# Retention's v turned at eviction, residual's copies beside attention, and more steps ahead of three uses

## The chip, the cores and the metric

The kernel runs on one core of one Trainium2 chip. A core has a matrix engine (TensorE, PE in the profile), a vector engine (VectorE, DVE), a scalar engine (ScalarE, ACT), GpSimd (POOL) and SyncE (SP), which issues most of the DMAs. The metric is the device time of one execution in microseconds. The profile's own execution is one of its own, beside the timed runs.

## The reference

One layer of a hybrid encoder over 1024 positions of width 2048, in float32. An RMSNorm of x is multiplied with one input matrix; its columns are retention's q, k, v and gate (8 heads of 128 each) and attention's q (8 heads), k, v (2 heads) and gate. The two branches are gated, put side by side, multiplied with an output matrix and added to x; a last RMSNorm follows.

```python
h = rms_norm(x, norm_w)
proj = h @ w_in
rq, rk, rv, rg, aq, ak, av, ag = jnp.split(proj, splits, axis=-1)
y_ret = retention_branch(rq, rk, rv, decay_fwd, decay_bwd, gn_w, gn_b) * silu(rg)
y_att = window_attention_branch(aq, ak, av, sink) * silu(ag)
return rms_norm(x + concat([y_ret, y_att]) @ w_out, final_norm_w)
```

Retention works on chunks of 128 positions, in both directions. Per head and chunk it needs the masked scores q k^T times v (`inner`), a running state that sums k^T v over the chunks with a decay (`kv_chunk`, `step`), and q times the state of the chunks before (`cross`). A GroupNorm over each head's 128 values follows.

## The kernel before, in words

**The projection sets the time.** It is a Strassen-like scheme: a unit is 512 columns of the input matrix and one half (part) of the sum over 2048 inputs, and it takes 7 products, listed in `PRODUCTS`. Each product of 4 x 2 groups of three float32r matmuls (`mm3`, L99 to L101) writes two PSUM banks. `PHASES` gives the order of the units: first part 0 of akv, aq0, aq1, rk0, rq0 (attention's k, v and q, and half of retention's k and q); then part 1 of these and of rv0, rk1, rq1, rv1; then part 0 of rv0, rk1, rq1, rv1 and of the gates; then part 1 of the gates. So retention's v, in rv0 (heads 0 to 3) and rv1 (heads 4 to 7), is made in two passes. `evict` takes a product from PSUM: for products 1, 6, 5 and 4 ScalarE copies the bank into a tile `ct` (L317), for 2, 7 and 3 VectorE adds the bank to a held tile (L92). Four of the seven give a finished quarter, which `store` puts into the list `stores`; `flush` issues them, in the last of the next product's four steps. The first pass writes plainly on SyncE's queue (L285), the second adds in memory on GpSimd's queue (L287). The tiles `ct` come from a ring of 8.

**Steps and jobs.** All else runs beside the projection as generators. `advance` counts one step of the projection (six matmuls of width 512) and then lets each job run up to its next `yield`; `idle(n)` is n steps. So the order of TensorE's, SyncE's and GpSimd's instructions is written out by hand: the jobs' instructions stand where their step is. `manual_schedule` names just these three engines. The instructions of VectorE and ScalarE are ordered by the planner of the Tile framework, which works through a simulated time and may put a later one first when it takes its inputs to be there; only `behind(...)` holds an instruction in the written order. Every engine then works through its own list in order.

**Jobs that matter here.** `attention` starts behind akv in phase 1 and, when its eight heads are done, runs `retention` and then `gating` as one job. `settled` counts a block as ready 8 steps after its last unit, which is also the time in which its stores land. `turn_v` (L752) fetches each v head 1 to 7 as two halves from `pr`, turns each on VectorE in blocks of 32x32 (`turn_half`, L152) and stores it into `vz`. `residual` (L1204) copies x into `res`, eight copies of 1 MB from memory to memory, one every 12 steps; the output projection adds on to `res` later.

**A retention head** (`head`). It waits until kT and qT are loaded and rotated (`fetch`, L779 to L796: load, rest some steps, then per half multiply, multiply, add on VectorE). It takes the scores (L840), waits for its v and until the head before is normalised (`while busy`), transposes kT (L567) into k_tok, starts the next head's kT, scales v (L859), forms the outer products (L872) and on VectorE the states (L884, L886), which are split into a rounded part and a rest, sH and sL (L88, L85). Then q is split (qhl), the next head's qT is started, and after an `idle` come `inner` (L920) and `cross`, which multiplies qhl with sH and sL (`mm3`) and adds it to y (L913). `normed` normalises y, turns it (L147), and stores it into `mix`. Head 0's v is no case of `turn_v`: `fetch_v` loads it and TensorE transposes it. The other heads' `fetch_v` is a `gather` of four DMAs (L161) from `vz`.

**Behind it.** `gating` loads `mix` and the gates, multiplies them (L1330 for attention's half, L1328 for retention's) and splits the operands (c) of the output projection, which begins when the last unit is done.

Of the kernel before, what the change touches and what calls it, by code (L numbers as in the profile page):

```python
# [9 lines left out]
F32 = mybir.dt.float32  # L10
# [8 lines left out]
P = 128  # L19
SQ = 32  # L20
S = 1024
# [4 lines left out]
RH = 8  # L26
# [17 lines left out]
BLOCKS = {  # L44
    "akv": 5120, "aq0": 4096, "aq1": 4608, "ag0": 5632, "ag1": 6144,
    "rk0": 1024, "rk1": 1536, "rq0": 0, "rq1": 512, "rv0": 2048, "rv1": 2560, "rg0": 3072, "rg1": 3584,
}
T_RQ, T_RK, T_RV, T_RG, T_AQ, T_AK, T_AV, T_AG = 0, 8, 16, 24, 32, 40, 42, 44
# [10 lines left out]
def hybrid_layer_kernel(  # L59
# [6 lines left out]
    nc = tc.nc  # L66
    x, w_in, w_out, out = x[0], w_in[0], w_out[0], out[0]
# [12 lines left out]
    def ax():  # L80
        return psp.tile([P, HALF], F32, name="ax", tag="ax", bufs=4)
# [9 lines left out]
    def add(dst, a, b):  # L91
        nc.vector.tensor_tensor(out=dst, in0=a, in1=b, op=ALU.add)  # L92
# [10 lines left out]
    def behind(it, ins):  # L103

        if it:
            tc.keep_in_program_order(ins)

    def blk(i, n=1):
        return slice(i * P, (i + n) * P)

    def half(i):
        return slice(i * HALF, (i + 1) * HALF)
# [9 lines left out]
    def start(job):  # L122
        if next(job, True) is None:
            jobs.append(job)
# [4 lines left out]
    def idle(n):  # L129
        for _ in range(n):  # L130
            yield
# [8 lines left out]
    pr = [dram.tile([P, S], F32, name=f"pr{i}") for i in range(52)]  # L140
    mix = [dram.tile([P, S], F32, name=f"mix{i}") for i in range(KT)]
    vz = [dram.tile([2, P, HALF], F32, name=f"vz{i}") for i in range(RH)]
    NB = P // SQ
# [6 lines left out]
    def turn_half(dst, src):  # L150

        nc.vector.transpose(out=dst.rearrange("p (b c i) -> p b c i", b=NB, i=SQ), in_=src.rearrange("p (c b i) -> p b c i", b=NB, i=SQ))  # L152

    def gather(dst, src):

        if len(src.shape) == 3:
            of = src.rearrange("m (a i) (b r) -> b i (m a) r", i=SQ, b=NB)
        else:
            of = src.rearrange("(a i) (b r) -> b i a r", i=SQ, b=NB)
        for b in range(NB):  # L160
            nc.sync.dma_start(out=dst[b * SQ:(b + 1) * SQ].rearrange("p (n r) -> p n r", r=of.shape[-1]), in_=of[b])  # L161

    def in_order(t):

        return t.rearrange("p (a c j) -> p c a j", a=NB, j=SQ)
# [19 lines left out]
    def ct():  # L185
        return wp.tile([P, HALF], F32, name="ct", tag="ct", bufs=8)
# [90 lines left out]
    done, seen = set(), set()  # L277
    comb = {}

    stores = []  # L280
# [29 lines left out]
    def evict(b, i, a, bank, held):  # L310

        def store(n, m, t):
            stores.append((b not in seen, pr[BLOCKS[b] // P + 2 * n + a][:, half(m)], t))

        if i in (1, 6, 5, 4):
            t = ct()
            nc.scalar.copy(out=t, in_=bank)  # L317
            if i == 4:
                store(1, 0, t)
            else:  # L320
                held[i, a] = t
        else:
            t = held.pop(({2: 1, 7: 5, 3: 6}[i], a))
            add(t, bank, t)
            store(*{2: (0, 0), 7: (1, 1), 3: (0, 1)}[i], t)
# [8 lines left out]
    def first_block(b, of):  # L334
# [3 lines left out]
        for m, order in ((0, QUARTERS), (1, QUARTERS[2:] + QUARTERS[:2])):  # L338
            for n, k in order:
# [30 lines left out]
                t += 1  # L370
        seen.add(b)
        on_done(0, b)

    def project(on_done, on_free):
# [187 lines left out]
    def transposed(src):  # L562

        for b in range(2):
            pt = ax()
            for t in range(4):
                nc.tensor.transpose(pt[:, blk(t)], src[:, blk(b * 4 + t)], ident)  # L567
            yield b, pt
# [5 lines left out]
    def settled(b):  # L574
        return b in done and clock[0] >= since[b] + 8

    def needs(*blocks):

        while not all(settled(b) for b in blocks):
            yield  # L580
# [166 lines left out]
        nc.vector.tensor_scalar(out=kd, in0=kd, scalar1=SCALE, scalar2=None, op0=ALU.mult)  # L747


    turned = set()  # L750

    def turn_v():  # L752
        for h in range(1, RH):
            yield from needs("rv" + str(h // 4))
            for m in range(2):
                f, z = ct(), ct()
                nc.sync.dma_start(out=f, in_=pr[T_RV + h][:, half(m)])
                yield from idle(6)
                turn_half(z, f)
                yield from idle(3)  # L760
                nc.sync.dma_start(out=vz[h][m], in_=z)
                yield
            turned.add(h)

    def retention():
        with right("ret") as ret:
            df = ret.tile([P, P], F32, name="df")
# [4 lines left out]
            kq, vs = {}, {}  # L772
# [3 lines left out]
            def fetch(name, c, h):  # L776

                t = ret.tile([P, S], F32, name=name, tag=name)
                nc.sync.dma_start(out=t, in_=pr[c + h])  # L779
                beside = []  # L780

                def pair(i):
                    beside.append(ret.tile([P, HALF], F32, name="rx", tag="sd" if h == 0 and c == T_RQ else "rx", bufs=2))
                    for r in (0, HP):
                        nc.sync.dma_start(out=beside[i][r:r + HP], in_=pr[c + h][HP - r:P - r, half(i)])

                for i in range(2):
                    pair(i)
                yield from idle(7 if h or c == T_RK else 11)
                for i in range(2):  # L790
                    u, b = t[:, half(i)], beside[i]
                    behind(h == 0, nc.vector.tensor_tensor(out=u, in0=u, in1=rot[:, 0, half(i)], op=ALU.mult))
                    yield
                    behind(h == 0, nc.vector.tensor_tensor(out=b, in0=b, in1=rot[:, 1, half(i)], op=ALU.mult))
                    add(u, u, b)
                    yield  # L796
                kq[name, h] = t

            def fetch_v(h):
                if h == 0:  # L800
                    yield from needs("rv0")
                    f = ret.tile([P, S], F32, name="vT", tag="vdq")
                    nc.sync.dma_start(out=f, in_=pr[T_RV])
                    yield from idle(5)
                    t = ret.tile([P, S], F32, name="v_tok")
                    for b, pt in transposed(f):
                        nc.scalar.copy(out=t[:, half(b)], in_=pt)
                        yield
                    vs[h] = [t[:, half(m)].rearrange("p (c a j) -> p c a j", a=NB, j=SQ) for m in range(2)]
                    return  # L810
                while h not in turned:
                    yield
                t = ret.tile([P, S], F32, name="v_tok")
                gather(t, vz[h])
                yield from idle(5)
                vs[h] = [in_order(t[:, half(m)]) for m in range(2)]

            def next_of(name, c, h):

                if h < RH:  # L820
                    yield from idle(2)
                    yield from needs(("rk" if c == T_RK else "rq") + str(h // 4))
                    yield from fetch(name, c, h)

            def head(h):
# [10 lines left out]
                for b in range(2):  # L836
                    sc = ax()
                    for t in range(4):
                        c = blk(4 * b + t)
# [57 lines left out]
                y = ret.tile([P, NT, P], F32, name="y", tag="y")  # L897
                bn = ret.tile([P, NT, 6], F32, name="bn")
                mv = ret.tile([P, NT, 2], F32, name="mv")
                yield from idle(2)  # L900

                def cross(c0):
                    cr = ax().rearrange("p (c d e) -> p c d e", d=2, e=P)
# [25 lines left out]
                if h + 1 < RH:  # L929
                    yield  # L930
                    start(fetch_v(h + 1))
# [28 lines left out]
            def heads():  # L960
                nc.gpsimd.dma_start(out=rot, in_=rot_r)
                while to_load:
                    yield
                yield from idle(8)
                yield
                start(next_of("kT", T_RK, 0))
                yield from idle(3)
                start(next_of("qT", T_RQ, 0))
                start(fetch_v(0))
                yield  # L970
                for h in range(RH):
                    yield from head(h)
                while len(finished) < RH:
                    yield
# [208 lines left out]
    def on_done(p, b):  # L1183
        if b in done:
            since.setdefault(b, clock[0])
        if p == 1 and b == "akv":
            start(attention())
        if p == 2 and b == "rv0":
            start(turn_v())
        if p == 2 and b == "rq1":  # L1190
            start(residual())


# [10 lines left out]
    def residual():  # L1204

        for t in range(NT):
            nc.sync.dma_start(out=res[t], in_=x[blk(t)])
            yield from idle(12)
# [276 lines left out]
    for u in range(len(OUT)):  # L1485
# [4 lines left out]
        for group in LAST if u == 3 else [(i,) for i in PRODUCTS]:  # L1490
# [13 lines left out]
            for at, (p, t, j, q) in enumerate(order):  # L1504
# [6 lines left out]
                bank, c = (X if p in ON_X else Y), comb[p]  # L1511
# [80 lines left out]
```

## Time and profile before

| | |
|---|---|
| Timed runs | 1531.01, 1532.34, 1531.01 us (median 1531.01) |
| The profiled execution | 1529.65 us, of it a span of 1527.9 us |
| Mean granted TensorE clock | 0.995 |
| TensorE busy | 1503.0 us (98%), 7286 matmul records |
| VectorE busy | 1086.0 us (71%) |
| ScalarE busy | 695.2 us (45%) |
| Attention beside the projection | about 330 to 655 us of the span |
| Retention beside the projection | about 665 to 1105 us |
| Output projection | from about 1211 us |

TensorE's busy share counts a matmul from issue to its modelled end, so matmuls in a row overlap; the spacing of their starts is their price. Where TensorE has idle time, or where its clock is below 1.00, time is lost. VectorE's share is a mean over stages in which it is nearly idle and others in which it never rests.

### The profile page before, as it was taken

The page shows a single profiled execution, that of the slowest core. Times are in us where ns is not written, and L with a number is a line of the kernel's source. Part 1 is how long each engine was busy: PE and PEld are TensorE (multiplying, and loading weights), DVE is VectorE, ACT ScalarE, POOL GpSimd, SP SyncE. Part 2 cuts the span into 40 slices and gives each one's busy share as a digit, 9 for nine tenths or more (in the row PEclk, how much of TensorE's full clock was granted, in tenths as well). Part 3 has the DMA queues.
Part 4 walks back from the last instruction along what each step waited for, and adds up shares of the span by engine and source line. Part 5 has one row for each costly group of instructions (what it writes and reads, how often), then busy time and mean ns, then how long its engine had stood idle before and what let it go on. Part 6 is the DMA issues. An engine that isn't in the chain of part 4 may idle for free.

```text
span 1527.9 us, 20264 instructions
## 1 busy us (share of the span) xinstructions
PE 1503.0 (98%) x7286; PEld 1263.7 (83%) x7286; DVE 1086.0 (71%) x1861; ACT 695.2 (45%) x1141; POOL 149.0 (10%) x169
## 2 busy tenths in 40 slices
PE   9999999999999999999999999999999999999997
PEld 7888888788888888888887888887888878888886
DVE  6896594557767576756977697768755966776766
ACT  7543462334545354533534453444444663542425
POOL 0000001111010000011111100001111102020001
PEclk9999999999999999999999999999999999999999
DMA  8288847889573425796787858589689699394656
GB/s 321 65 284 307 310 165 196 231 197 253 155 207 125 138 83 182 283 309 166 162 203 194 230 164 262 169 268 325 174 234 262 150 217 226 83 212 165 214 175 254
DMA packets 167447, 317.86 MB, mean 208 GB/s; under 512 B 14865, under 2 KB 84913, under 8 KB 158514
## 3 DMA queue, kind: packets, MB, share of 16 engines
q1 hardware_dynamic: 143298, 265.69, 51.9%
q0 software_dynamic: 19728, 36.71, 15.7%
q10 hardware_dynamic: 4320, 14.17, 2.8%
q8 instruction: 57, 0.93, 0.2%
q14 instruction: 44, 0.36, 0.1%
HBM read 196.70 MB, written 128.19 MB: 213 GB/s over the span
## 4 chain that ended last, share of the span: by engine, by line
PE 70%; issue 11%; DVE 11%; DMA 6%; SPq 1%; POOL 1%; ACT 0%; ACTq 0%; DVEq 0%; POOLq 0%
PE pj L101 17%; PE pj L99 17%; PE pj L100 17%; PE ax L100 5%; PE ax L101 5%; PE ax L99 5%; DMA kT<-pr 3%; DVE wL L85 2%; DMA xt<-in_x_dram 1%; DVE ct L92 1%; PE ax L645 1%; DMA pr<-ct 1%; DVE c L85 1%; DVE st L886 1%; DVE sL L85 1%
## 5 line engine op out<-in xcount | busy, mean ns | idle before, releaser
L99 PE MATMUL pj<-c,wH 128*128 128x512 f32 x1444 | 576.3, 399 | 0.0
L101 PE MATMUL pj<-c,wL 128*128 128x512 f32 x1440 | 563.7, 391 | 2.5 <-DVE wL L85 2.5
L100 PE MATMUL pj<-c,wH 128*128 128x512 f32 x1444 | 564.1, 391 | 0.0
L101 PEld LDWEIGHTS pj<-c,wL 128*128 128x128 f32 x1440 | 270.9, 188 | 62.9 <-DVE wL L85 4.8
L100 PEld LDWEIGHTS pj<-c,wH 128*128 128x128 f32 x1444 | 272.3, 189 | 50.5 <-DVE c L1000 0.3
L99 PEld LDWEIGHTS pj<-c,wH 128*128 128x128 f32 x1444 | 272.3, 189 | 50.2 <-issue 0.3
L85 DVE TENSOR_TENSOR wL<-a,wH 128x1024 fp32r<-128x1024 f32 x157 | 191.4, 1219 | 117.0 <-ACT wH L88 114.8
L88 ACT CAST wH<-a 128x1024 fp32r<-128x1024 f32 (+1 forms) x159 | 166.2, 1045 | 216.9 <-PE pj L100 112.0
L317 ACT COPY ct<-pj 128x512 f32<-128x512 f32 x192 | 111.5, 585 | 209.7 <-PE pj L101 208.8
L287 POOL DMA_DIRECT2D pr<-ct x104 | 91.9, 952 | 622.9 <-DVE ct L92 502.4
L92 DVE TENSOR_TENSOR ct<-pj,ct 128x512 f32<-128x512 f32 x164 | 108.9, 685 | 48.6 <-PE pj L101 47.8
L85 DVE TENSOR_TENSOR wL<-s,wH 128x1024 fp32r<-128x1024 f32 x56 | 68.3, 1219 | 50.6 <-ACT wH L88 50.3
L100 PE MATMUL pj<-wL,c 128*128 128x512 f32 x224 | 87.4, 390 | 1.2 <-DVE wL L85 1.1
L99 PE MATMUL pj<-wH,c 128*128 128x512 f32 x224 | 87.2, 389 | 0.0
L101 PE MATMUL pj<-wH,c 128*128 128x512 f32 x224 | 87.1, 389 | 0.0
L100 PE MATMUL ax<-wL,c 128*128 128x512 f32 x208 | 81.2, 390 | 0.1
L101 PE MATMUL ax<-wH,c 128*128 128x512 f32 x208 | 81.0, 389 | 0.0
L99 PE MATMUL ax<-wH,c 128*128 128x512 f32 x208 | 80.9, 389 | 0.0
L88 ACT CAST wH<-s 128x1024 fp32r<-128x1024 f32 x56 | 59.0, 1053 | 22.1 <-DVE s L95 9.9
L88 ACT CAST sH<-st 128x256 fp32r<-128x256 f32 x56 | 22.7, 406 | 76.6 <-DVE st L886 42.2
L100 PEld LDWEIGHTS pj<-wL,c 128*128 128x128 f32 x224 | 42.1, 188 | 10.6 <-DVE wL L85 2.0
L99 PEld LDWEIGHTS pj<-wH,c 128*128 128x128 f32 x224 | 42.1, 188 | 8.8
(246 smaller groups left out, 2036.3 us busy)
## 6 DMA issues: line engine op xcount, KB each, us to landing
a<-in_w_in_dram SPq DMA_DIRECT2D x103, 512.0 KB, 5.9
kept<-c SPq DMA_DIRECT2D x28, 1024.0 KB, 7.9
c<-kept SPq DMA_DIRECT2D x28, 1024.0 KB, 9.3
pr<-ct SPq DMA_DIRECT2D x110, 256.0 KB, 5.6
pr<-ct POOLq DMA_DIRECT2D x104, 256.0 KB, 6.0
a<-in_w_out_dram SPq DMA_DIRECT2D x18, 512.0 KB, 5.2
rx<-pr SPq DMA_DIRECT2D x64, 128.0 KB, 6.8
ysrc<-pr ACTq DMA_DIRECT2D x16, 512.0 KB, 5.9
```

The source lines that it names most:

```text
L85: return nc.vector.tensor_tensor(out=dst, in0=src, in1=high.bitcast(F32), op=ALU.subtract)
L88: behind(pinned, nc.scalar.copy(out=dst_h, in_=src))
L92: nc.vector.tensor_tensor(out=dst, in0=a, in1=b, op=ALU.add)
L99: nc.tensor.matmul(po, aH, bH, start=first, stop=False, **kw)
L100: nc.tensor.matmul(po, aH, bL, start=False, stop=False, **kw)
L101: nc.tensor.matmul(po, aL, bH, start=False, stop=last, **kw)
L287: nc.gpsimd.dma_start(out=dst, in_=t, accum_op=ALU.add)
L317: nc.scalar.copy(out=t, in_=bank)
L645: nc.tensor.transpose(pt[:, blk(j)], s[:, blk(j)], ident)
L886: nc.vector.scalar_tensor_tensor(out=cur[:, d], in0=prev[:, d], scalar=cd[:, d * RH + h:d * RH + h + 1], in1=p, op0=ALU.mult, op1=ALU.add)
```

## The change

There are five edits.

1. `evict`: where a finished quarter belongs to rv0 or rv1, it is turned by `turn_half` into a second `ct` tile, and that is stored, into `vz` instead of `pr`, in the first pass and, adding, in the second.
2. `turn_v` and its start are gone, and `fetch_v` does for head 0 what it does for the others: wait for the block, gather, rest 5 steps.
3. `fetch`: kT rests 10 steps between its load and its rotation where it rested 7; qT keeps its 7 (11 for head 0).
4. `head`: 3 idle steps instead of 2 between the split of q and `inner` and `cross`.
5. `residual` starts when rq0 is done in phase 1 (step 284) instead of rq1 in phase 2 (step 480).

```diff
@@ evict
         def store(n, m, t):
-            stores.append((b not in seen, pr[BLOCKS[b] // P + 2 * n + a][:, half(m)], t))
+            c = BLOCKS[b] // P + 2 * n + a
+            if b in ("rv0", "rv1"):
+                z = ct()
+                turn_half(z, t)
+                stores.append((b not in seen, vz[c - T_RV][m], z))
+            else:
+                stores.append((b not in seen, pr[c][:, half(m)], t))
@@ turn_v
-    turned = set()
-
-    def turn_v():
-        for h in range(1, RH):
-            yield from needs("rv" + str(h // 4))
-            for m in range(2):
-                f, z = ct(), ct()
-                nc.sync.dma_start(out=f, in_=pr[T_RV + h][:, half(m)])
-                yield from idle(6)
-                turn_half(z, f)
-                yield from idle(3)
-                nc.sync.dma_start(out=vz[h][m], in_=z)
-                yield
-            turned.add(h)
@@ fetch
-                yield from idle(7 if h or c == T_RK else 11)
+                yield from idle(10 if c == T_RK else 7 if h else 11)
@@ fetch_v
-                if h == 0:
-                    yield from needs("rv0")
-                    f = ret.tile([P, S], F32, name="vT", tag="vdq")
-                    nc.sync.dma_start(out=f, in_=pr[T_RV])
-                    yield from idle(5)
-                    t = ret.tile([P, S], F32, name="v_tok")
-                    for b, pt in transposed(f):
-                        nc.scalar.copy(out=t[:, half(b)], in_=pt)
-                        yield
-                    vs[h] = [t[:, half(m)].rearrange("p (c a j) -> p c a j", a=NB, j=SQ) for m in range(2)]
-                    return
-                while h not in turned:
-                    yield
+                yield from needs("rv" + str(h // 4))
                 t = ret.tile([P, S], F32, name="v_tok")
                 gather(t, vz[h])
                 yield from idle(5)
@@ head
-                yield from idle(2)
+                yield from idle(3)
@@ on_done
-        if p == 2 and b == "rv0":
-            start(turn_v())
-        if p == 2 and b == "rq1":
+        if p == 1 and b == "rq0":
             start(residual())
```

## The prediction

> **What bounds the kernel now.** I read the page's busy times first.
>
> ```profile
> span 1527.9 us, 20264 instructions
> ...
> PE 1503.0 (98%) x7286; PEld 1263.7 (83%) x7286; DVE 1086.0 (71%) x1861; ACT 695.2 (45%) x1141; POOL 149.0 (10%) x169
> ```
>
> TensorE is busy for 1503.0 of 1527.9 us, so a change can win only the 24.9 us in which it is idle, what a lowered clock costs, and TensorE instructions that go away. The table by stages says where that lies; its columns are the stretch, its length, then busy time and count for PE, PEld, DVE, ACT and POOL, the granted clock, DMA share and GB/s.
>
> ```profile
> 784.00:843.00 59.00, 53.16 (x280) 44.63 (x279) 44.28 (x93) 25.75 (x47) 10.78 (x11) 0.99 0.77 198
> 843.00:894.00 51.00, 50.31 (x264) 42.96 (x263) 38.97 (x87) 21.68 (x39) 2.57 (x1) 0.98 0.67 204
> 944.00:995.00 51.00, 49.63 (x264) 42.31 (x264) 42.77 (x98) 21.41 (x40) 3.05 (x1) 1.00 0.65 202
> 995.00:1048.00 53.00, 51.15 (x262) 43.26 (x261) 41.29 (x95) 22.59 (x41) 2.45 (x1) 0.97 0.86 279
> 1100.00:1150.00 50.00, 50.00 (x222) 41.41 (x221) 30.68 (x31) 21.39 (x29) 8.81 (x10) 1.00 0.79 207
> 435.00:492.00 57.00, 57.00 (x311) 49.95 (x310) 43.60 (x120) 32.38 (x75) 1.74 (x2) 1.00 0.46 139
> 492.00:592.00 100.00, 100.00 (x521) 86.25 (x520) 62.90 (x142) 45.37 (x95) 0.00 (x0) 1.00 0.33 108
> 592.00:647.00 55.00, 55.00 (x294) 48.08 (x293) 40.52 (x108) 29.39 (x67) 0.00 (x0) 1.00 0.77 273
> 1211.00:1234.00 23.00, 21.65 (x93) 16.91 (x92) 22.83 (x21) 13.83 (x17) 1.74 (x2) 1.00 0.98 208
> ```
>
> From 784 to 1048 us retention's heads run beside the projection, and TensorE is idle there for 5.84 + 0.69 + 1.37 + 1.85 = 9.75 us (length less PE busy of the first four rows). The clock below 1.00 costs 59 x 0.01 + 51 x 0.02 + 53 x 0.03 = 3.2 us more. This stage, 13 us, is what the change can win. In attention (435 to 647 us) TensorE never stops. The fifth row gives the step of the text: 50 us for 222 matmuls is 0.225 us each, and a step of the projection is 6 of them, 1.35 us.
>
> Who ends TensorE's waits in retention (690 to 1060 us; total, times, longest), and what VectorE waits for there:
>
> ```profile
> PE ax L100 <- DVE sL L85: 4.2, 5, 1.3
> PE ax L99 <- ACT sH L88: 3.0, 3, 2.1
> PE ax L101 <- DVE qhl L85: 1.6, 2, 0.8
> PE pj L101 <- DVE wL L85: 1.0, 2, 0.5
> ```
>
> ```profile
> DVE kT L792 <- DMA kT<-pr: 30.6, 7, 6.5
> DVE ct L152 <- DMA pr<-ct: 4.3, 1, 4.3
> DVE ct L152 <- DMA ct<-pr: 4.0, 2, 3.7
> DVE qT L792 <- DMA qT<-pr: 3.3, 1, 3.3
> ```
>
> All but 1.0 us is one place: `cross`, where a head's q (qhl) meets its states (sH, sL). Those come late because VectorE stood still, up to 6.5 us, for the next head's kT. The timeline of VectorE shows one such head, that of TensorE its end:
>
> ```profile
> 817.92 1.23 DVE L85 TENSOR_TENSOR wL<-s,wH 128x1024 fp32r<-128x1024 f32 x1 [1.68 <-ACT wH L88]
> 825.65 1.29 DVE L792 TENSOR_TENSOR kT<-kT,rot 128x512 f32<-128x512 f32 x2 [6.50 <-DMA kT<-pr]
> 826.86 0.68 DVE L794 TENSOR_TENSOR rx<-rx,rot 128x512 f32<-128x512 f32 x1
> 827.46 1.28 DVE L92 TENSOR_TENSOR ct<-pj,ct 128x512 f32<-128x512 f32 x2
> 828.66 1.21 DVE L85 TENSOR_TENSOR wL<-a,wH 128x1024 fp32r<-128x1024 f32 x1
> 829.79 0.48 DVE L884 COPY st<-ax 128x128 f32<-128x128 f32 x2
> ...
> 837.09 0.68 DVE L92 TENSOR_TENSOR ct<-pj,ct 128x512 f32<-128x512 f32 x1
> ```
>
> ```profile
> 787.88 0.33 PE L100 MATMUL ax<-sL,qhl 128*128 128x128 f32 x1 [1.31 <-DVE sL L85]
> ...
> 839.12 0.33 PE L99 MATMUL ax<-sH,qhl 128*128 128x128 f32 x1 [2.06 <-ACT sH L88]
> 840.15 0.33 PE L100 MATMUL ax<-sL,qhl 128*128 128x128 f32 x1 [0.71 <-DVE sL L85]
> 841.29 0.33 PE L101 MATMUL ax<-sH,qhl 128*128 128x128 f32 x1 [0.81 <-DVE qhl L85]
> ```
>
> VectorE is idle until 825.65, then works without a break until `cross` is reached at 839. One thing more is to be seen here. In the code the rotation of kT (L792) stands 3 + 7 steps behind the k_tok transposes, the head's state updates (L884) 7 steps behind them. On the chip L792 came first. VectorE's order is the planner's (only TensorE, SyncE and GpSimd are written out by hand), and it put L792 where it thought the load had landed.
>
> **The change part by part.** The sum is made against the profiled execution: 1529.65 us, of which 1527.9 are the span; the median shown is 1531.01, 1.4 above it.
>
> ```profile
> L152 DVE STREAM_TRANSPOSE ct<-ct x14: 682/702/711, 705.7 to 996.9; 128x512 f32<-128x512 f32 x14
> ```
>
> ```profile
> 756.67 0.89 PE ax L840 x8
> ```
>
> ```profile
> L567 PE MATMUL ax<-ident,vT 128*128 128x128 f32 x8 | 1.2, 272 | 0.0
> ```
>
> *Head 0's v.* Its 8 transposes leave TensorE. Eight 128x128 matmuls issued in a row take 0.89 us (the L840 piece), so: -0.9. The two copies on ScalarE and one load go too, and four gathers come in their place, as for every other head. Head 0 gets v two steps earlier.
>
> *No turn_v.* 14 transposes of 0.70 us (9.8 us of VectorE), their 8.3 us of waits, 14 loads and 14 stores on SyncE's queue leave retention. VectorE's order around kT stays, and the waits that were counted are kT's: I take -0.5, with 0 and -3 as bounds (-3 where two turns less per head, 1.4 us, come off the two crossings that stay late).
>
> *Turns at eviction.* 32 transposes of the same shape come: 16 in the first pass of rv0 and rv1, beside attention, 16 in the second. No store or byte is added; each store waits for one more VectorE instruction, on SyncE's queue in the first pass and on GpSimd's in the second, and it uses a second of the 8 `ct` buffers. In the first pass a unit of 55 to 57 us gets 8 x 0.70 = 5.6 us and has 13.4 and 14.5 us of idle VectorE (435 and 592 rows) to hide it. Without that cover it is 11.2 us. The turns come in pairs of 1.4 us ahead of the operands that TensorE wants next, so I take +1, bounds 0 and +5. The second pass of rv1 lies at 784 to 843 us, where nothing is idle once kT has landed: the turns behind the additions of product 7 (827.46) and product 3 (the second of them at 837.09) stand in the burst ahead of 839, 2.8 us, less the removed turn of this head, 0.7: +2.1, bounds 0 and +5.6 (all eight).
>
> *One step more ahead of inner and cross* (idle 2 to 3). TensorE's order is by hand, so `cross` really comes 1.35 us later behind the states and qhl. Each crossing's wait falls by at most that: 1.31 by 1.3, the 3.58 at 839 to 841 by 1.35, and the 0.69, 1.37 and 1.85 us of the other three windows by 0.7, 1.35 and 1.35. Together -6.0. Bounds 0 (VectorE slides as well) and -8.8 (all three kinds). With the waits half of the 3.2 us of lowered clock goes: -1.6, bounds 0 and -3.2. The clock is below 1.00 in three of the windows, though no wait in them is longer than 2.1 us. [...]
>
> *Three more steps for kT.* By hand only the place in the program moves. As the timeline shows, L792 runs long before its place in the program, so the stall that ends at 825.65 stays: 0. The bound is the other reading, below.
>
> *The price of the step.* I counted the steps of `head` from the code. From one k_tok to the next it is 27 before: the chain qhl, idle 2, load of qT, 7 steps, rotation, scores. `normed` frees y at step 26, just ahead of it. With the added step it frees y at 27, so `while busy` holds the next head a step: 28. Head 0 starts two steps sooner (438 for 440), head 7 at 634 for 629, and retention ends at step 665 instead of 659. So `gating`, which follows it, starts 6 x 1.35 = 8.1 us later, while the output projection begins at the same step, 732. This is what gating's end looks like in VectorE's timeline, and the only wait it leaves TensorE with (1200 to 1240 us):
>
> ```profile
> 1175.80 1.23 DVE L1330 TENSOR_TENSOR ysrc<-ysrc,yt 128x1024 f32<-128x1024 f32 x1 [5.83 <-DMA yt<-mix]
> ...
> 1188.76 1.22 DVE L1330 TENSOR_TENSOR ysrc<-ysrc,yt 128x1024 f32<-128x1024 f32 x1
> 1189.90 1.22 DVE L85 TENSOR_TENSOR c<-ysrc,c 128x1024 fp32r<-128x1024 f32 x1
> ...
> 1230.90 1.22 DVE L85 TENSOR_TENSOR wL<-a,wH 128x1024 fp32r<-128x1024 f32 x1
> ```
>
> ```profile
> PE pj L100 <- DVE wL L85: 1.1, 1, 1.1
> ```
>
> From the last product (1188.76) to 1232 VectorE never rests, and TensorE catches up with it. Moved by up to 8.1 us, the block's end moves by less, since other operands fill the hole in front: +3, bounds 0 and +8.
>
> *Residual's copies.* The eight move from 788 to 945 us to behind step 284, one per 12 steps, that is to 435 to about 590 us:
>
> ```profile
> L1207 SPq DMA_DIRECT2D res<-in_x_dram x8: 500/521/713, 787.9 to 944.8; - x8
> ...
> DMA to landing us min/median/max: 7.3/8.5/10.0
> ```
>
> At 8.5 us in 16 to 20 they meet a DMA share of 0.46 and 0.33. Loads behind them on SyncE's queue land later, but the weights are asked for a unit ahead: 0, bounds -1 (kT lands sooner) and +2.
>
> Sum: -0.9 - 0.5 + 1 + 2.1 - 6.0 - 1.6 + 3 = -2.9 by the takings alone. Two of them lean high: the turns in this burst and the late gating are each charged as if no planner moved anything around them. Halving those two, as the middle between bound 0 and the taking, gives -5.4. I forecast between the two, -4.2 us: 1525.4 in the profile, **1526.8 us** in the median.
>
> **The rivals.**
>
> *A. Nothing to be seen.* The waits move rather than go: VectorE still stands for kT, the eviction's turns lengthen the burst by the 2.8 us that the step gives back over two heads, attention pays 2, gating 3. Then -0.9 - 6.0 + 2.8 + 2 + 3 = +0.9, less 0.5 for turn_v and 1.0 of clock: -0.6, 1530.4. For it: the 30.6 us of kT waits are left as they are by my own reading. Against: three of five crossings wait 1.37 us or less, and these vanish with one step.
>
> *B. kT's wait goes as well.* If the planner follows the program, three steps take 4.05 us off each of the seven waits; the rest of 9.75 us (3.7) and of the clock (1.6) would go on top: 1526.8 - 5.3 = 1521.5, and 1517.5 where neither gating nor attention costs its 3 + 1. For it: 30.6 us in 7 heads are 4.4 each, about three steps. Against: L792 ahead of L884 in the timeline. [...]
>
> *C. Slower: gating becomes the bound.* One mechanism, at 1188 to 1240 us: the head's 28th step delays the last product by the full 8.1 us, the 12 operand splits behind it stand ahead of wL in VectorE's order, and TensorE waits all of it at steps 732 to 744. It decides from about 6 us of delay on, if the crossings win less than 4: 1531 + 8 - 4 = 1535. For it: VectorE is 22.83 of 23.00 us busy in the 1211 row. Against: the 5.83 us hole ahead of 1175.80, which a later product leaves free for other operands.
>
> **How the numbers follow.** 0.2%, about 3 us, is what can be told from no change. Forecast 0.40; B 0.14; A 0.28; C 0.18. Faster: forecast and B, less the edge of the forecast near 1528, 0.52. Same: A and that edge, less A's edge, 0.28. Slower: C and A's edge, 0.20. The forecast's own range is 1521 to 1531. To leave out 2 in 10 the range takes B's and C's times with little beyond: 1516 to 1537.
>
> **What would show it.** Right: waits of `ax` on sH, sL and qhl between 690 and 1060 us down from 8.8 to about 3; no L152; L792 still behind 25 to 30 us of kT; scores (L840) of neighbouring heads 28 steps apart; the last L1330 of attention's half some 6 us later, with up to 4 us of wait for wL behind it. Wrong: kT's wait gone (B); waits on wL of 8 us at 1211 to 1240 (C); waits in attention, where there are none now; a second pass of rv1 that stops TensorE for more than its 5.84 us.

## The result, and the profile after

The changed kernel takes 1518.67 us in the median (1518.10 to 1520.17), the kernel before 1531.01 us (1530.22 to 1532.34): ratio 0.992, 95% interval 0.9903 to 0.9937, faster by 12.3 us. The forecast was 1526.8 us, 4.2 us faster. The side is right and the time lies in the stated range of 1516 to 1537 us, but the forecast size is a third of what came.

The page of the changed kernel, its span and busy times:

```profile
span 1516.3 us, 20238 instructions
...
PE 1498.1 (99%) x7278; PEld 1260.4 (83%) x7278; DVE 1097.8 (72%) x1879; ACT 695.9 (46%) x1139; POOL 148.1 (10%) x169
```

Lines have moved: the rotation is L783 now (L792), its scores L819 (L840), `inner` L899 (L920), attention's half of gating L1307 (L1330). The table by stages of the changed kernel (stretch, length, busy time and count of PE, PEld, DVE, ACT, POOL, granted clock, DMA share, GB/s):

```profile
784.00:843.00 59.00, 59.00 (x323) 50.91 (x322) 50.00 (x103) 26.28 (x46) 10.56 (x11) 1.00 0.67 148
843.00:894.00 51.00, 51.00 (x272) 43.55 (x271) 42.27 (x98) 23.11 (x42) 1.66 (x1) 1.00 0.51 155
944.00:995.00 51.00, 51.00 (x270) 43.26 (x269) 42.40 (x96) 22.49 (x40) 1.92 (x1) 1.00 0.52 162
995.00:1048.00 53.00, 53.00 (x283) 45.43 (x282) 45.23 (x92) 25.50 (x46) 6.75 (x4) 1.00 0.92 315
435.00:492.00 57.00, 56.81 (x308) 49.57 (x308) 46.17 (x126) 31.77 (x73) 1.74 (x2) 1.00 0.60 196
1211.00:1260.00 49.00, 44.77 (x190) 36.25 (x189) 24.26 (x25) 25.50 (x29) 5.68 (x7) 0.97 0.91 227
690.00:1060.00 370.00, 370.00 (x1956) 316.06 (x1955) 302.50 (x623) 171.10 (x298) 39.61 (x35) 1.00 0.65 181
```

In retention TensorE no longer stops at all: of its waits between 690 and 1060 us the view has no row left, where before it had 9.8 us, and the clock is 1.00 in all four stretches. Attention loses 0.19 us. A wait behind 1211 us has grown from 1.1 us to 3.7. Who ends VectorE's waits in retention (690 to 1060 us; total, times, longest), and TensorE's behind it (1060 to 1290 us):

```profile
DVE wL L85 <- ACT wH L88: 28.5, 16, 5.4
DVE kT L783 <- DMA kT<-pr: 17.4, 6, 4.9
```

```profile
PE pj L100 <- DVE wL L85: 4.2, 2, 3.7
```

VectorE's stalls for kT have shrunk from 30.6 to 17.4 us, and the 8.3 us for turn_v's loads are gone. Its waits for ScalarE's half of the weight splits (wH) are now the largest, but TensorE stands still for none of them here.

The cleanest account is the place of the output projection's first matmul in TensorE's timeline, first before, then after:

```profile
1211.20 0.39 PE L99 MATMUL ax<-wH,c 128*128 128x512 f32 x1
```

```profile
1195.72 0.39 PE L99 MATMUL ax<-wH,c 128*128 128x512 f32 x1
```

Up to there 1211.20 - 1195.72 = 15.5 us are won. From there to the end of the span it was 1527.9 - 1211.2 = 316.7 us and is 1516.3 - 1195.7 = 320.6, so 3.9 us are given back. The difference is the span's 11.6 us.

### The profile page after: what moved, and what is told of

Read it like the earlier page. It is cut to its first block, busy times and chain, and to the rows that moved or that the text cites. A ratio compares the mean times of both kernels' runs of the same rounds, so it can differ in the third digit from the quotient of the medians.

```text
span 1516.3 us, 20238 instructions
## 1 busy us (share of the span) xinstructions
PE 1498.1 (99%) x7278; PEld 1260.4 (83%) x7278; DVE 1097.8 (72%) x1879; ACT 695.9 (46%) x1139; POOL 148.1 (10%) x169
## 4 chain that ended last, share of the span: by engine, by line
PE 79%; issue 9%; DVE 5%; DMA 5%; ACT 1%; SPq 0%; POOL 0%; ACTq 0%; POOLq 0%; DVEq 0%
PE pj L101 20%; PE pj L100 20%; PE pj L99 20%; PE ax L101 5%; PE ax L100 5%; PE ax L99 5%; PE ax L851 2%; DMA xt<-in_x_dram 1%; DVE wL L85 1%; PE ax L651 1%; DMA pr<-ct 1%; PE ax L819 1%; PE ax L899 1%; DVE c L85 1%; DMA q<-pr 1%
## 5 line engine op out<-in xcount | busy, mean ns | idle before, releaser
L287 POOL DMA_DIRECT2D pr<-ct x88 | 78.0, 957 | 539.2 <-DVE ct L92 412.4
L641 ACT ACTIVATE s<-s,nm 128x385 f32<-128x385 f32 (+1 forms) x64 | 37.6, 589 | 28.5 <-DVE nm L636 25.7
```

Of the source, the lines that this page charges most:

```text
L287: nc.gpsimd.dma_start(out=dst, in_=t, accum_op=ALU.add)
L641: nc.scalar.activation(out=s[:, 0:w + 1], in_=s[:, 0:w + 1], func=AF.Exp, scale=-1.0, bias=nm, accum_out=den)
```

## The experiments

The theories at the start, as the expectations name them. Theory 1: the step ahead of `cross` takes the waits away. Theory 2: fewer transfers and loads on SyncE's queue do it (kT lands earlier, nothing of turn_v stands in VectorE's list), and the step is not needed. Theory 3: kT's longer rest does nothing. Theory 4: the 28-step head makes gating late, and that is the wait behind 1200 us.

Each ratio is to the kernel before, from runs on the same chip; the other columns are read from the one profiled execution of each kernel, which can lie 2 or 3 us from its median, and that of a_copies_late 5 us (1525.02 us, the slowest of its six runs, for a median of 1519.88). "Steps" is the length of a head in steps of the projection; "idle" is length less PE busy of 690 to 1060 us, "output begins" the first matmul as above, "rest" the span less that.

| kernel | steps | ratio, 95% interval | idle | output begins | rest |
|---|---|---|---|---|---|
| before | 27 | 1 | 9.75 | 1211.2 | 316.7 |
| changed | 28 | 0.992 (0.9903-0.9937) | 0.00 | 1195.7 | 320.6 |
| b_step | 28 | 0.9994 (0.9983-1.0006) | 5.32 | 1208.8 | 317.2 |
| b_turn | 27 | 0.9996 (0.9987-1.0006) | 10.50 | 1212.0 | 319.0 |
| b_copies | 27 | 0.9973 (0.9963-0.9984) | 9.04 | 1207.8 | 316.1 |
| b_kt10 | 27 | 1.0011 (1.0000-1.0021) | 10.36 | 1215.4 | 316.4 |
| a_step2 | 27 | 0.9988 (0.9977-0.9999) | 5.70 | 1207.6 | 320.1 |
| a_kt7 | 28 | 0.9936 (0.9912-0.9960) | 1.30 | 1198.2 | 320.3 |
| a_copies_late | 28 | 0.9932 (0.9911-0.9952) | 4.00 | 1202.6 | 320.6 |
| a_norm | 27 | 1.0006 (0.9994-1.0018) | 7.77 | 1211.3 | 319.5 |
| a_per28 | 28 | 0.9962 (0.9949-0.9974) | 4.48 | 1202.6 | 321.5 |
| a_29 | 29 | 1.0026 (1.0012-1.0039) | 3.17 | 1214.8 | 316.1 |
| a_last | 28 | 0.9925 (0.9910-0.9940) | 0.10 | 1197.0 | 322.6 |
| b_gate6 | 27 | 1.0036 (1.0022-1.0050) | 10.06 | 1215.3 | 320.7 |

### One part of the change alone, added to the kernel before

**b_step**, the step alone:

```diff
-                yield from idle(2)
+                yield from idle(3)
```

> The kernel before with the extra step alone (idle 2 to 3 ahead of inner and cross), nothing else. Theory 1 (the step takes the crossings' waits away): waits of ax on sH, sL and qhl between 690 and 1060 us fall from 8.8 to 3 or less, TensorE's wait for wL near 1216 us rises from 1.1 to about 4, and the time is 3 to 6 us below before. Theory 2 (fewer transfers take the waits away, the step is not needed): the waits stay above 5 us, the gating's price of 3 to 5 us comes on top, and the time is at or up to 4 us above before.

The step does to the crossings what the prediction said. TensorE's waits in 690 to 1060 us (total, times, longest), and behind 1060:

```profile
PE ax L100 <- DVE sL L85: 3.1, 4, 1.0
PE pj L101 <- DVE wL L85: 1.7, 3, 0.6
```

```profile
PE pj L101 <- DVE wL L85: 1.8, 1, 1.8
PE ax L100 <- DVE wL L85: 0.8, 1, 0.8
```

Waits on sH, sL and qhl fall from 8.8 to 3.1 us, close to the "about 3" that the prediction named. Yet the time stays: 0.9994. Other waits came, for the projection's own weight splits (wL): behind 1060 us TensorE is idle for 3.76 us where before had 1.35, and behind the wait at 1174.86 the clock is lowered, 0.66 from 1175 to 1180 us (last section). What VectorE waits for changes too, though no load was touched:

```profile
DVE kT L792 <- DMA kT<-pr: 21.5, 6, 6.9
```

Before had 30.6 us here. Theory 1 is right about the place and wrong about the time.

**b_turn**, edits 1 and 2 alone (the diff of `evict`, `turn_v` and `fetch_v` above):

> The kernel before with retention's v turned at eviction and stored turned, no turn_v, head 0's v gathered; the step stays 2, kT's rest 7, residual's copies late. Theory 1 (the step does it): waits of ax on sH, sL and qhl stay at 6 us or more, and the time is within 3 us of before (0.9 us of TensorE's transposes goes in any case). Theory 2 (the relief of SyncE's queue and of VectorE does it): VectorE's waits for kT fall from 30.6 to about 20 us, those waits of ax fall to 3 us or less, and the time is 6 to 10 us below before. My prediction's charge of 2.1 us for the turns in the burst at 784 to 843 us would show as TensorE idle there for more than 5.84 us.

No gain: 0.9996. Its own rows, stage and VectorE's wait, then what TensorE waits for behind 1060 us:

```profile
784.00:843.00 59.00, 54.69 (x295) 46.43 (x294) 47.44 (x102) 26.58 (x47) 11.35 (x11) 1.00 0.75 197
```

```profile
DVE kT L783 <- DMA kT<-pr: 27.8, 7, 7.2
```

```profile
PE pj L100 <- DVE wL L85: 3.2, 1, 3.2
PE pj L101 <- DVE wL L85: 2.4, 2, 1.5
```

The turns in the burst of rv1's second pass cost nothing: 59.00 - 54.69 = 4.31 us idle, below the 5.84 of before. But kT's waits stay (27.8) and the crossings still wait 6.2 us, so theory 2 falls, and the wait of over 3 us for wL behind 1200 us is already there, with 27-step heads and gating as early as before.

**b_copies**, edit 5 alone:

```diff
+        if p == 1 and b == "rq0":
+            start(residual())
...
-        if p == 2 and b == "rq1":
-            start(residual())
```

> The kernel before with residual's eight copies beside attention and nothing else. Theory 2a (the copies slow kT's loads): VectorE's waits for kT fall from 30.6 us by 5 or more, waits of ax fall by 2 to 4 us, time 2 to 5 us below before. Theory 1 and the prediction: kT's waits fall by less than 5 us, time within 1.5 us of before. Either way attention from 435 to 647 us stays without waits.

Faster by 4 us, but not in the way that theory 2a named: kT's waits are 30.0 us, and TensorE's idle time falls by only 9.75 - 9.04 = 0.7 us. The rest is the clock: in the four stretches of the prediction's first rows, b_copies has 1.00 where before has 0.99, 0.98, 1.00 and 0.97. Two stretches behind crossings of before, and the two behind the longest crossing waits of b_copies:

```profile
843.00:846.00 3.00, 3.00 (x12) 2.44 (x11) 3.00 (x7) 0.00 (x0) 0.00 (x0) 0.66 0.97 231
1040.00:1044.00 4.00, 4.00 (x14) 3.20 (x13) 4.00 (x11) 0.00 (x0) 0.00 (x0) 0.62 1.00 263
```

```profile
841.00:845.00 4.00, 4.00 (x25) 3.51 (x25) 4.00 (x8) 0.03 (x1) 0.81 (x1) 1.00 0.98 178
988.00:992.00 4.00, 4.00 (x25) 3.55 (x24) 4.00 (x16) 0.00 (x0) 0.00 (x0) 1.00 0.53 157
```

In these stretches before has a clock near 0.64, b_copies 1.00. The matmul counts can't be compared, since b_copies' stretches hold narrower matmuls as well; the spacing of the projection's 128x512 matmuls can, first before, then b_copies:

```profile
843.72 0.63 PE L100 MATMUL pj<-c,wH 128*128 128x512 f32 x1
844.15 0.63 PE L101 MATMUL pj<-c,wL 128*128 128x512 f32 x1
```

```profile
842.11 0.39 PE L101 MATMUL pj<-c,wL 128*128 128x512 f32 x1
842.33 0.40 PE L99 MATMUL pj<-c,wH 128*128 128x512 f32 x1
```

They start 0.43 us apart in the one and about 0.23 in the other. At the two crossings behind which the clock of before fell, b_copies waits less: 0.71 + 0.81 = 1.5 us for 3.58 (839 to 841 us), and 0.81 for 1.86 (1035 to 1038 us). But its own longest crossing wait, 1.20 + 0.77 = 1.97 us at 985 and 986 us, is longer than the 1.86 of before and leaves the clock alone. Why is not explained by any row.

**b_kt10**, kT's rest 7 to 10:

```diff
-                yield from idle(7 if h or c == T_RK else 11)
+                yield from idle(10 if c == T_RK else 7 if h else 11)
```

> The kernel before with kT's rest raised from 7 to 10 steps and nothing else. Theory 3 (the planner has put the rotation ahead of its place in the program anyway): the rotation stands at the same place of VectorE's order for heads 1 to 6, VectorE's waits for kT stay at 27 us or more, time within 1.5 us of before. Rival B of the prediction: each of seven waits is 4.05 us shorter, kT's waits fall below 10 us, time about 5 us below before.

```profile
DVE kT L792 <- DMA kT<-pr: 31.6, 7, 7.4
```

Theory 3 holds: 31.6 for 30.6 us. The planner had put the rotation ahead of its place in the program, and three steps more do not reach it. Rival B's mechanism falls with this.

The four ratios multiplied give 0.9974, 4 us, nearly the forecast. The whole change gives 12.3. So some 8 us lie in the parts together.

### One part taken away from the changed kernel

**a_step2** (`idle(3)` back to `idle(2)`):

> The changed kernel with the step taken back (idle 3 to 2 ahead of inner and cross). Theory 1 (the step removes the crossings' waits): waits of ax on sH, sL and qhl come back with 5 us or more between 690 and 1060 us, the wait for wL near 1216 us falls from 3.7 to about 1, time 0 to 3 us above the changed kernel, 1518 to 1522. Theory 2 (with kT landing about 2 us earlier and no turn_v the step is no longer needed; in the changed kernel the crossings have 14 to 19 us behind kT's rotation where before had 7 to 15): waits stay below 2 us, the wait for wL falls all the same, time 4 to 6 us below the changed kernel, 1513 to 1515.

```profile
690.00:1060.00 370.00, 364.30 (x1914) 309.88 (x1913) 298.37 (x621) 167.90 (x292) 45.68 (x35) 1.00 0.64 176
1060.00:1290.00 230.00, 223.70 (x1009) 184.85 (x1008) 150.95 (x183) 110.25 (x140) 39.49 (x44) 0.99 0.84 208
```

The ratio goes back to 0.9988: without the step nearly all of the gain is lost. Theory 2 is out, and theory 1 had the sign but a fraction of the size. The waits come back in retention (5.70 us). The one behind 1200 us should have gone, by theory 1 and by the prediction's price of a late gating; it stays:

```profile
PE pj L100 <- DVE wL L85: 3.9, 2, 3.2
```

**a_kt7** (the rest of kT back to 7) and **a_copies_late** (residual started where it was before):

> The changed kernel with kT's rest back at 7 steps. Theory 3 (the planner sets the place of the rotation, the program's step does not; the rest alone added to before gave 1.0011): within 1.5 us of the changed kernel, VectorE's waits for kT 15 to 21 us. Rival B: these waits rise by 4 us for each of six heads and the time by 4 us or more.

> The changed kernel with residual's copies back in retention. If the gain is the sum of its parts (the copies alone gave 0.9973, 4.1 us): 4 us above the changed kernel, 1522 to 1524. If the parts share one cover (theory 1: the step alone is enough for the crossings): kT lands 2 us later, 8.5 to 9.5 us behind its issue in place of 7, TensorE's waits for the states stay below 2 us, time within 2 us of the changed kernel. If the parts need each other (theory 2): those waits come back with 4 us or more, time 6 us or more above.

Both stay within the interval of the changed kernel, 0.9936 and 0.9932. Either edit can be taken away alone. VectorE's waits for kT without the three steps are 18.5 us, for 17.4. With the copies back kT lands 8.3 to 10.8 us behind its issue for heads 3 to 6, where the changed kernel has 6.8 to 9.1, and VectorE's waits for it are 20.7 us, for 17.4; still no wait for the states returns, as theory 1 has it; the profiled execution shows one other wait, 3.59 us for wL at 837.01. That both can go at once was not run.

One more thing is in these numbers. b_step and a_copies_late both have the step and the late copies, and differ by edits 1 to 3, the turned v and kT's rest: 0.9994 and 0.9932, 9.5 us. Alone, edits 1 and 2 gave 0.9996 and edit 3 gave 1.0011. So the step is worth next to nothing without them, and kT's rest is hardly what it needs, since a_kt7 does without it. What in the turned v helps was not separated: head 0 starts two steps sooner, and 14 turns with 8.3 us of waits leave VectorE's list in retention.

**a_norm**, one step less in `normed`, so that a head takes 27 steps while the step ahead of `cross` is kept:

```diff
                         yield
-                yield from idle(2)
+                yield from idle(1)
                 for b in range(2):
```

> The changed kernel with one idle step less in normed (2 to 1), so that y is free a step earlier and a head takes 27 steps again, with the step ahead of cross kept. Theory 4 (gating starts 6 to 8 steps later only because of the 28th step, and this costs the wait of 3.7 us for wL near 1216 us with the clock behind it): that wait falls to about 1, time 3.5 to 5.5 us below the changed kernel, 1513 to 1515. Otherwise (the wait for wL has another source, or a shorter head brings crossing waits back): within 2 us of it or above.

This was meant as an improvement and is the run that tells most. The whole gain is gone: 1.0006. TensorE's waits in 690 to 1060 us:

```profile
PE pj L101 <- DVE wL L85: 5.7, 6, 2.2
PE ax L819 <- DVE qT L92: 1.4, 1, 1.4
PE ax L100 <- DVE sL L85: 0.6, 2, 0.5
```

The crossings are fine (0.6 us): here the step ahead of them does its work. What waits is the projection itself, for its weight splits. So the edit `idle(2)` to `idle(3)` is two things, a later `cross` and a longer head, and the gain needs the longer head, which the prediction booked as a price. It is not enough by itself: b_step has 28 steps and the later `cross` and gains nothing.

### The length of a head

A unit of the projection is 7 products of 4 steps, 28 steps. That suggests a theory 5: a head of 28 steps meets the same evictions and splits of the unit every time, one of 27 or 29 drifts.

**a_per28**: a 28-step head without the later `cross`.

```diff
-                yield from idle(3)
+                yield from idle(2)
...
-                yield from idle(2)
+                yield from idle(3)
                 for b in range(2):
```

> The changed kernel with the step ahead of inner and cross taken back (idle 3 to 2) and one step added in normed instead (second idle 2 to 3): cross stands as near behind the states as before the change, but a head still takes 28 steps, as many as a unit of the projection has (7 products of 4 steps). Theory 5 (what counts is the period: each head meets the same places of the unit): no or few waits of ax on sH, sL and qhl, at most 2 us between 690 and 1060 us, heads 48.8 us apart, time within 3 us of the changed kernel, 1516 to 1522. Theory 1 (what counts is the step between the states and cross): as with the step taken back alone, waits of 4 us or more there, time 1526 to 1531.

```profile
PE ax L101 <- DVE qhl L85: 2.5, 4, 0.8
PE ax L99 <- ACT sH L88: 0.8, 1, 0.8
PE ax L100 <- DVE sL L85: 0.7, 1, 0.7
```

0.9962, between the two theories. Against a_step2 the longer head alone is worth 0.0026, 4 us. The crossings wait 4.0 us, none over 0.9, and a step of 1.35 us covers each of these waits; with it the changed kernel has none and is 0.0042, 6.4 us, faster. Four kernels have all the other edits and differ in these two things alone. With 27 steps the ratio is 0.9988 without the later `cross` (a_step2) and 1.0006 with it (a_norm); with 28 steps it is 0.9962 (a_per28) and 0.992. So the later `cross` wins nothing in the shorter head and 6.4 us in the longer one: both halves are needed.

**a_29**, one step more (`normed`'s second idle 2 to 3, the rest as changed):

> The changed kernel with one step more in normed (second idle 2 to 3), so that a head takes 29 steps: the step ahead of cross is kept, VectorE has still more time for each head, but heads move by one step a head against the unit of 28. Theory 5 (period): waits come back in the retention stage, 3 us or more between 690 and 1060 us, time 1522 to 1531. Slack theory (a longer head is simply more room for VectorE): no waits there; gating starts 8 steps, 11 us, later, so the waits for wL behind 1190 us grow from 4 to 6 us or more, time 1520 to 1526.

```profile
690.00:1060.00 370.00, 366.83 (x1930) 312.41 (x1929) 299.06 (x617) 166.91 (x291) 43.85 (x35) 1.00 0.65 179
1060.00:1290.00 230.00, 218.84 (x977) 179.23 (x976) 148.14 (x183) 106.90 (x137) 38.82 (x43) 0.98 0.76 194
```

```profile
PE pj L99 <- ACT wH L88: 4.2, 2, 2.6
PE pj L101 <- DVE wL L85: 3.5, 2, 1.9
```

The second fence holds its waits behind 1060 us. At 1.0026 it is slower than before, beyond what either theory had named. In 690 to 1060 us some waits return (3.17 us), as the period theory wants, but fewer than at 27 steps with the same edits; behind 1060 us, where the last head and gating now fall 8 steps later than in the changed kernel, the idle time is 230.00 - 218.84 = 11.2 us where the changed kernel has 4.24. So 28 is the best of the three lengths. Whether by its equal place in each unit or by being long enough without being late is not settled; b_step, also of 28 steps but from head 0 on two steps later in the unit, still has 5.32 us of idle time.

What the length changes can be read in two timelines, VectorE's first rotation of a head's kT and TensorE's first `cross` behind it. Distance in us, for the kT of heads 2 to 6:

| kernel | steps | head 2 | 3 | 4 | 5 | 6 |
|---|---|---|---|---|---|---|
| before | 27 | 15.5 | 13.5 | 12.7 | 10.7 | 9.8 |
| a_step2 | 27 | 13.8 | 10.7 | 8.7 | 10.8 | 12.7 |
| a_norm | 27 | 16.8 | 12.6 | 10.1 | 10.4 | 12.6 |
| a_per28 | 28 | 14.2 | 14.4 | 13.1 | 13.8 | 15.3 |
| b_step | 28 | 15.4 | 15.5 | 14.3 | 12.3 | 17.4 |
| changed | 28 | 18.7 | 17.1 | 14.2 | 15.5 | 15.2 |
| a_29 | 29 | 17.6 | 14.5 | 17.4 | 13.8 | 14.8 |

At 27 steps it shrinks to 9 or 10 us, in the longer heads of this table it stays above 12, and the changed kernel has the most of it in the mean. This is the room in which VectorE, released from its stall for kT, makes the states and the splits. How much of it is needed differs from head to head: before waits 3.6 us behind 13.5 and nothing behind 10.7, and a_copies_late, with 28 steps, has one of 10.7 and no crossing that waits. So the distance alone does not decide; that the place in the unit is the rest of it is a guess that no run shows.

### The price behind 1200 us

**b_gate6**, six idle steps between retention and gating of the kernel before:

```diff
         yield from retention()
+        yield from idle(6)
         yield from gating()
```

> The kernel before with six idle steps put between retention and gating, so that gating starts 8.1 us later and all else stays. Theory 4 (the late gating is what TensorE waits for at the output projection's start, as the prediction's term of +3 and its rival C have it): waits for wL behind 1150 us rise from 1.1 to 4 us or more, time 3 to 8 us above before. Against it (the kernels with 27 steps and the turned v wait there too, with gating as early as before): waits stay below 2.5 us, time within 2 us of before.

```profile
690.00:1060.00 370.00, 359.94 (x1875) 305.85 (x1874) 290.06 (x612) 160.57 (x282) 39.50 (x33) 0.99 0.73 208
1060.00:1290.00 230.00, 225.16 (x1020) 186.08 (x1019) 152.42 (x189) 114.72 (x149) 38.67 (x43) 0.99 0.81 212
```

```profile
PE pj L100 <- DVE wL L85: 3.3, 2, 3.2
```

Retention is as before (10.06 us idle), behind it 4.84 us are idle for 1.35, and the time is 5.4 us up (1.0036). In that kernel a late gating does cost time: more than the +3 that the prediction took, within its bounds of 0 and 8.

**a_last**: the last head's `normed` cut by four steps, so that by the program gating starts 5.4 us earlier and heads stay 28 steps long.

```diff
-                yield from idle(2)
+                yield from idle(2 if h + 1 < RH else 0)
...
-                yield from idle(3)
+                yield from idle(3 if h + 1 < RH else 1)
```

> The changed kernel with the last head's normed cut by four idle steps (second idle 2 to 0, the one before its stores 3 to 1), so that the 28-step heads stay as they are and gating starts 5.4 us earlier. Theory 4: the wait of 3.7 us for wL near 1216 us falls to 1 or less with the halved clock behind it, time 3 to 5.5 us below the changed kernel, 1513 to 1516. If gating's start does not set that wait (but the planner's order of the last splits): within 2 us of the changed kernel.

Nothing is won: 0.9925. The wait is even 4.3 us, and VectorE's timeline shows why. Splits of the output's weights (wL<-r), first in the changed kernel, then in a_last:

```profile
1204.76 1.22 DVE L85 TENSOR_TENSOR wL<-r,wH 128x1024 fp32r<-128x1024 f32 x1
...
1215.10 1.22 DVE L85 TENSOR_TENSOR wL<-r,wH 128x1024 fp32r<-128x1024 f32 x1
```

```profile
1211.21 1.22 DVE L85 TENSOR_TENSOR wL<-r,wH 128x1024 fp32r<-128x1024 f32 x1
...
1213.48 1.22 DVE L85 TENSOR_TENSOR wL<-r,wH 128x1024 fp32r<-128x1024 f32 x1
```

TensorE waits for the second in the one (its matmul comes at 1216.38) and for the first in the other (1212.49). With gating earlier the planner puts other work ahead, and the first split moves back by 6.5 us. Gating did move: measured from the output projection's first matmul, its first and third load of `mix` go out 93.2 and 81.6 us ahead, where the changed kernel has 90.8 and 76.1.

The other kernels bear this out. Before has these loads 101.8 and 81.6 us ahead. In b_step they are late, at 94.6 and 73.5, and no wait behind 1200 us is above 0.8 us. In b_turn, a_step2 and a_norm they are earlier than before, at 104.8 and 90.0, and TensorE waits 3.2, 3.2 and 2.5 us in one piece for wL. So this wait doesn't need a late gating and doesn't always follow one; b_gate6 shows that it can. Theory 4 falls for the changed kernel: what its wait shows is a split that VectorE, busy for 21.97 of the 22.00 us from 1195 to 1217 us, takes up late in its list. No kernel tried has a lower ratio than the changed one.

## Why the prediction was right and wrong

- **Where the time could be won**: right. It was retention's stage, and the output projection begins 15.5 us earlier. The 13 us that the prediction allowed it were a little low. Length less PE busy leaves out what a matmul's modelled end covers: a matmul lasts 0.39 us in the record and the next one starts 0.23 us behind it, so each of the 12 waits hides about 0.16 us, by estimate 2 us in all.
- **Head 0's v**: its 8 matmuls are gone (7286 to 7278 records); nothing tells the -0.9 apart.
- **Turns at eviction**: +1 in attention came as 0.19 us, and the +2.1 in rv1's second pass did not come, in b_turn either. Both were too high.
- **One step ahead of cross**: -6.0 was right for the waits. b_step takes 5.7 us off them, and a_per28, which lacks just this step at the same length of head, is 6.4 us slower. As a term of time it holds only there: alone the step wins nothing, because other waits follow (b_step), and neither does it in heads of 27 steps (a_norm for a_step2). Of the lowered clock in this stage all 3.2 us went (the clock is 1.00 in all four stretches of the changed kernel), for the -1.6 taken; the rows that showed it were right to be charged.
- **kT's three steps**: 0, right (b_kt10, a_kt7), by the reason given, the planner's order. Rival B had the nearest time, 1521.5 or 1517.5, but not by its mechanism: kT's waits fell to 17.4 us without these steps' doing. They fell all the same, and the prediction named 25 to 30 us as its sign: that sign failed. The added step of the head alone brings them to 21.5 (b_step).
- **Residual's copies**: 0 between -1 and +2 was wrong alone, -4.1 us (b_copies), by the clock; in the changed kernel taking them back costs nothing that can be told (a_copies_late).
- **The price of the step**: this is where the mechanism failed. The 28 steps were counted right, and the prediction saw only a cost, +3 at gating. A cost of that size came (3.9 us), but it can't be put down to the late gating: b_turn, a_step2 and a_norm give back 2.3 to 3.4 us with gating earlier than before, and b_step 0.5 us with a late one. What was missed is the gain: with the same step ahead of `cross` and 27 steps (a_norm) the kernel is 0.0086, 13 us, slower than with 28.
- **The sum**: the terms were added as if each stood alone, and measured alone the parts do add up to 4 us. That the forecast's -4.2 is so near to this is luck, since the two get there by different terms: in the forecast the step wins and the copies nothing, in the runs the copies alone win and the step alone nothing. So that the side came right is in part luck as well. Together the parts do not add: VectorE's order is one list, and a part that removes one wait leaves the next. The turned v was measured with the step only in company of the copies or of kT's rest; whether the step with the copies alone would do as well was not run.
- **Rival A** is out: the waits went. **Rival C**'s wait is there with 3.7 us of its 8, and does not decide.

## What to carry to other kernels

Where jobs run beside a periodic main stream, work out the period of each against that of the stream, and try the length that equals it as well as its neighbours, before pricing an added step as a delay; here 28 was best of three, and why is open. Where a planner orders an engine, test the parts together as well as alone: four parts worth 4 us singly were worth 12 in one kernel, and a part may be needed for something other than what it was written for, as the step was for the length of the head. A step taken away at the end of a stage is no gain in itself where that planner decides what fills the room.

## What the runs showed of the hardware

In b_step TensorE's clock fell behind a wait of 1.77 us. Its timeline of TensorE (start, duration, and in brackets the idle time before):

```profile
1174.86 0.50 PE L101 MATMUL pj<-c,wL 128*128 128x512 f32 x1 [1.77 <-DVE wL L85]
1175.19 0.40 PE L99 MATMUL pj<-c,wH 128*128 128x512 f32 x1
...
1176.74 0.63 PE L99 MATMUL pj<-c,wH 128*128 128x512 f32 x1
1177.16 0.63 PE L100 MATMUL pj<-c,wH 128*128 128x512 f32 x1
...
1179.72 0.43 PE L100 MATMUL pj<-c,wH 128*128 128x512 f32 x1
1179.99 0.40 PE L101 MATMUL pj<-c,wL 128*128 128x512 f32 x1
```

Behind the wait the matmuls first start 0.23 us apart, the pace of the other timelines here. Then, 1.5 us later, eight of them come 0.43 us apart, and the pace is back at 1179.72. The granted clock was 0.66 from 1175 to 1180 us and 1.00 in the 5 us that follow. The slow stretch lasts 3.4 us and costs 8 x 0.2 = 1.6 us, about as much as the wait. In the changed kernel a wait of 3.67 us was followed by the same, with a clock of 0.63 from 1216.4 to 1221 us. The length of the wait does not decide alone: in b_copies a crossing with 1.97 us of idle time (985 and 986 us) and in b_turn a single wait of 1.9 us (for sH, in retention) had no slow stretch behind them. The clock was 1.00 in b_copies from 985 to 992 us, and in b_turn in each of the five stretches from 784 to 1048 us, which hold 10.18 of its 10.50 us of idle time. So in this kernel a wait of 2 us may be priced, by estimate, at 2 or, by the 1.6 us above, at 3.6 us.
